# Two heads' score products on the two halves of the array's rows, operands split once for both heads

## The chip, the cores and the metric

One core of one Trainium2 chip runs the whole program. The metric is device microseconds of one execution. Five engines take part: TensorE (PE; its weight loads are shown as PEld), VectorE (DVE), ScalarE (ACT), GpSimd (POOL) and SyncE (SP), which issues the DMAs.

## What is computed

Three transformer-like layers over 512 tokens of width 1024, in float32. Two "hybrid" layers and one "second" layer:

```python
def hybrid_layer(x, ...):                      # twice
    u = rms_norm(x, g) @ w_in
    aq, ak, av, cu, rq, rk, rv, rg = split(u)
    y_att  = chunk_attention(aq, ak, av, rel_bias)   # 6 heads of 64
    y_conv = conv_module(cu, ...)                    # 31 taps over 256 channels
    y_ret  = retention(rq, rk, rv, rg)               # 6 heads of 64
    x = x + rms_norm(concat(y_att, y_conv, y_ret) @ w_out)
    return x + rms_norm(square(relu(rms_norm(x) @ w_up)) @ w_down)

def second_block(x, ...):                      # once
    q, k, v, u, gates = split(rmsnorm(x) @ w_in)
    o = diff_attention(q, k, v, lam)                 # 8 heads, two score maps of 64 each
    s = s5_layer(u, ...)                             # a state space model
    h = x + (g_attn * (o @ w_attn_proj) + g_ssm * (s @ w_ssm_proj)) @ w_out
    return h + (silu(gate) * val of causal_dwconv(rmsnorm(h) @ w_up)) @ w_down
```

A score map is the product of a head's queries and keys, a contraction over 64 features. There are 12 attention heads, 12 retention heads and 8 differential heads with two maps each: 40 maps, or 20 pairs.

## The kernel before

**Precision.** TensorE multiplies in its faster float32r format. To keep float32 accuracy, each operand is split into a high part, rounded to float32r by ScalarE (or VectorE), and a low part, the rest, made by VectorE (or GpSimd). A product over 128 features is three matmuls: high by high, high by low, low by high.

**Scores before.** A score map contracts over 64 features only, half of the array's 128 rows. `stack` (line 1060) puts a head's high parts in one half of the rows and its low parts in the other; `dup` (line 1076) writes the other operand's high parts into both halves of one tile and its low parts into both halves of another. Two matmuls over 128 rows then give all four products of a map. For a pair of heads `stack` makes two tiles (two ScalarE and two VectorE instructions on 64 partitions) and `dup` four tiles (four and four).

**Tiles of scores.** `att_head` (line 1167) handles one head: for each of four blocks of 128 queries, one PSUM tile with 256, 256, 384 and 512 columns, evicted by a VectorE instruction that adds the bias and takes the maximum; then exponentials, normalisation, transposes (`p_trans`), and the product with V (`pv_pair`). Two heads of a pair are separate tasks, the second put 1709 ns later (`ATTV`). `diff_head` (line 1790) does the same for the two maps of a head in one task. `ret_pair` (line 1279) does the two heads of a retention pair one after the other: for each, three PSUM tiles that hold 512, 384 and twice 256 columns.

**Order of the work.** The program is recorded first (`Trace`), each instruction with a due time, and a planner (`order`, line 443) then lays it out by simulated time. `cost` (line 682) gives it the duration of each instruction. Due times run back through the dependencies: an instruction is due before each user of its result, by that user's cost and 100 ns. Each engine takes the ready instruction that is due first. The main stream of projections has the due times of TensorE's own progress `T`. Scores, transposes and the like are side tasks (`Side`), created at the current `T`, and a `yield n` moves the due times of what follows by n. All side tasks share four PSUM tiles (`pss`, line 833), the main stream has four others. `room` (line 609) keeps enough of them for what stands earlier in the program. The planner's order is then fixed: each engine issues in that order and waits on semaphores. The matmuls of side tasks and of the main stream so share one queue on TensorE.

All instructions are issued through one line (642), so that the profile's groups are told apart by tile names: `stk`, `khi` and `klo` are the stacked and duplicated operands, `row` the scores, `pthi` and `ptlo` the split transposed probabilities, `whi` and `wlo` weights of the main stream, `ps` a PSUM tile, `cm` the identity of a transpose, `ucm` and `gt` operands of the state space model, which is computed with plain float32 matmuls over 64 rows.

Of the kernel before, what the change touches and what calls it, by code (L numbers as in the profile page):

```python
# [10 lines left out]
F32 = mybir.dt.float32  # L11
# [6 lines left out]
P = 128  # L18
S = 512
# [205 lines left out]
class View:  # L225
    """A view of a tile that is traced before the tile is placed."""
# [103 lines left out]
class DramView(View):  # L330
    """A view of a tile in DRAM: taken as a whole."""
# [20 lines left out]
class Pool:  # L352
    """Equal slots, which the order of instructions deals out to tiles. Each is a pool of one buffer."""
# [46 lines left out]
class Trace:  # L400
    """Records instructions with the time by which each is wanted, orders them, and issues them."""
# [280 lines left out]
def cost(eng, method, kw_, op):  # L682
# [6 lines left out]
    if eng == "tensor":  # L689
# [119 lines left out]
class Builder:  # L809
# [132 lines left out]
    # ---------------------------------------------------------------- norms  # L942
# [116 lines left out]
    # ---------------------------------------------------------------- attention helpers  # L1059
    def stack(self, ps, scale=None):  # L1060
        nc = self.nc
        out = []
        for e in range(2):
            t = self.s2(F32R, "stk")
            a, b = (slice(0, 64), slice(64, 128)) if e == 0 else (slice(64, 128), slice(0, 64))
            if scale is None:
                nc.scalar.copy(t[a, :], ps[a, :])
                nc.vector.tensor_tensor(t[b, :], ps[a, :], t[a, :].bitcast(F32), op=ALU.subtract)
            else:
                nc.scalar.activation(t[a, :], ps[a, :], AF.Copy, scale=scale)  # L1070
                nc.vector.scalar_tensor_tensor(t[b, :], ps[a, :], scale, t[a, :].bitcast(F32),
                                               op0=ALU.mult, op1=ALU.subtract)
            out.append(t)
        return out

    def dup(self, ps):
        nc = self.nc
        hs, ls = [], []
        for e in range(2):
            a = slice(64 * e, 64 * e + 64)  # L1080
            hi, lo = self.s2(F32R, "khi"), self.s2(F32R, "klo")
            for b in (a, slice(64 - 64 * e, 128 - 64 * e)):
                nc.scalar.copy(hi[b, :], ps[a, :])
            for b in (slice(0, 64), slice(64, 128)):
                nc.vector.tensor_tensor(lo[b, :], ps[a, :], hi[a, :].bitcast(F32), op=ALU.subtract)
            hs.append(hi)
            ls.append(lo)
        return hs, ls
# [12 lines left out]
    def v_pack(self, src):  # L1101
        """V of six heads, each as 64 columns of high parts and 64 of low parts."""
# [11 lines left out]
    def pv_pair(self, h, pts, V, y):  # L1114
        """One head's output, from the products with the high and the low parts of V below each other."""
# [24 lines left out]
    def p_split(self, parts):  # L1140
        """High and low parts by blocks of keys: 512, 384 and twice 256 columns, the last with a block of zeros."""
        out = []
        for src, off in parts:
            n = src.shape[1]
            hi, lo = self.s2(F32R, "pthi"), self.s2(F32R, "ptlo")
            if off:
                for z in (hi, lo):
                    self.nc.gpsimd.memset(z[:, :off].bitcast(F32), 0.0)
            self.split(src, hi[:, off:off + n], lo[:, off:off + n])
            out.append((hi, lo))  # L1150
        last = out.pop()
        return out + [tuple(z[:, 256:512] for z in last), tuple(z[:, 0:256] for z in last)]

    def p_trans(self, rows):
        nc = self.nc
        parts = []
        for kts, off in (((0,), 0), ((1,), 0), ((3, 2), P)):
# [6 lines left out]
            parts.append((ps[:, :n], off))  # L1164
        return self.p_split(parts)

    def att_head(self, l, h, q, khi, klo, toe, V, dst):
        nc = self.nc
        p, e = h // 2, h % 2
        st = self.st()  # L1170
        rows = self.rows(self.s2(name="row")[:, :256])
        for qt in range(NT):
            n = P * (qt + 1)
            N = max(n, 256)
            ps = self.ps()
            nc.tensor.matmul(ps[:, :N], q[:, qt * P:(qt + 1) * P], khi[:, :N], start=True, stop=False)
            nc.tensor.matmul(ps[:, :N], q[:, qt * P:(qt + 1) * P], klo[:, :N], start=False, stop=True)
            nc.vector.tensor_tensor_reduce(out=rows[qt][:, :n], in0=ps[:, :n], in1=toe[:, S - n:S], scale=1.0, scalar=-3e38,
                                           op0=ALU.add, op1=ALU.max, accum_out=st[:, qt:qt + 1])
        nc.vector.tensor_scalar(st[:, 4:8], st[:, 0:4], -1.0, None, op0=ALU.mult)  # L1180
        for qt in range(NT):
            n = P * (qt + 1)
            nc.scalar.activation(rows[qt][:, :n], rows[qt][:, :n], AF.Exp, bias=st[:, 4 + qt:5 + qt],
                                 accum_out=st[:, 8 + qt:9 + qt])
        yield 50
        nc.vector.reciprocal(st[:, 12:16], st[:, 8:12])
        for qt in range(NT):
            n = P * (qt + 1)
            nc.vector.tensor_scalar(rows[qt][:, :n], rows[qt][:, :n], st[:, 12 + qt:13 + qt], None, op0=ALU.mult)
        yield 50  # L1190
        pts = self.p_trans(rows)
        yield 50
        y, hi, lo = dst
        self.pv_pair(h, pts, V, y)
        self.mixc[p] = self.mixc.get(p, 0) + 1
        if self.mixc[p] == 2:
            self.split(y, hi, lo)
            self.mix[p] = hi, lo

    # ---------------------------------------------------------------- conv module  # L1200
# [48 lines left out]
    # ---------------------------------------------------------------- retention  # L1249
# [29 lines left out]
    def ret_pair(self, p, q, k):  # L1279
# [7 lines left out]
        ks = self.stack(pss[0])  # L1287
        qh, ql = self.dup(pss[1])
        yield 50
        y = self.s2(name="ry")  # L1290
        for e in range(2):
            h = 2 * p + e
            parts = []
            for kts in ((0,), (1,), (3, 2)):
                ps = self.ps()
                n = 0
                for kt in kts:
                    q0 = 256 if kt == 3 else P * kt
                    o = ps[:, n:n + S - q0]
# [780 lines left out]
```

## Time and profile before

| | |
|---|---|
| median of 3 executions | 2181.93 us (2181.4 to 2184.87) |
| profiled execution, first to last instruction | 2185.0 us |
| TensorE matmuls busy | 2065.8 us, 95% of the span |
| VectorE, ScalarE, GpSimd busy | 64%, 42%, 34% |
| mean granted TensorE clock | 0.983 of full speed |
| score matmuls (`khi,stk` and `klo,stk`) | 320 |

The profiled execution's own time is its span; no time around it is recorded. A matmul's shown duration is longer than its place in the queue, because matmuls overlap: where TensorE is saturated, the distance from one start to the next is the price. Retention and attention of the first hybrid layer lie between about 113 and 300 us, those of the second between 740 and 960 us, differential attention between 1430 and 1700 us.

### The profile page before, as it was taken

What the parts mean: (1) busy time and instruction counts of PE and PEld (TensorE: products, weight loads), DVE (VectorE), ACT (ScalarE), POOL (GpSimd) and SP (SyncE); (2) the same over time, 40 slices, a digit from 0 to 9 for tenths busy, and PEclk for the clock granted to TensorE, in tenths of its full rate; (3) what the DMA queues carried; (4) which work ended last, traced back from release to release, by engine and by line L of the source; (5) the groups of instructions that cost most, each with busy time, mean ns of one, the idle gap of its engine ahead of it and who ended that gap; (6) DMA issues with size and microseconds to landing.
All of it is one profiled execution on the core that took longest, in us unless ns stands there. A gap on an engine that the chain in (4) does not pass through costs nothing. (4 is left out here: it accounts for less than half of the span.)

```text
span 2185.0 us, 27033 instructions
## 1 busy us (share of the span) xinstructions
PE 2065.8 (95%) x9964; PEld 1711.6 (78%) x9964; DVE 1395.2 (64%) x2131; ACT 928.5 (42%) x1521; POOL 745.5 (34%) x858
## 2 busy tenths in 40 slices
PE   7789989899999799989999998999999999999999
PEld 7777878778888777788888877677777788888887
DVE  6999596344457999573444464379888646655545
ACT  3267544232234267454222344456578324433332
POOL 3663357980004663210000115764643431000000
PEclk9999999999999999999999999999999999999999
DMA  5223233332333224133332346222224533333222
GB/s 176 80 78 123 87 116 109 128 127 87 97 114 97 87 68 135 49 107 97 96 97 77 115 133 201 79 80 68 92 82 135 169 96 97 97 96 97 87 87 77
DMA packets 85556, 225.16 MB, mean 103 GB/s; under 512 B 10416, under 2 KB 20400, under 8 KB 85424
## 3 DMA queue, kind: packets, MB, share of 16 engines
q1 hardware_dynamic: 85424, 223.43, 32.4%
q8 instruction: 79, 1.29, 0.3%
q14 instruction: 53, 0.43, 0.1%
HBM read 204.25 MB, written 19.14 MB: 102 GB/s over the span
## 5 line engine op out<-in xcount | busy, mean ns | idle before, releaser
L642 POOL TENSOR_TENSOR wlo<-wraw,whi 128x1024 fp32r<-128x1024 f32 (+1 forms) x156 | 374.5, 2408 | 1068.3 <-ACT whi L642 824.9
L642 ACT CAST whi<-wraw 128x1024 fp32r<-128x1024 f32 (+1 forms) x323 | 330.4, 1029 | 726.7 <-PE ps L642 592.1
L642 PE MATMUL ps<-hhi,whi 128*128 128x512 f32 (+1 forms) x1488 | 506.8, 370 | 7.3 <-DVE acc L642 3.1
L642 PE MATMUL ps<-hlo,whi 128*128 128x512 f32 (+1 forms) x1488 | 504.8, 370 | 5.6 <-DVE hlo L642 5.6
L642 PE MATMUL ps<-hhi,wlo 128*128 128x512 f32 (+1 forms) x1488 | 504.3, 369 | 0.3 <-DVE wlo L642 0.3
L642 PEld LDWEIGHTS ps<-hhi,whi 128*128 128x128 f32 x1488 | 272.4, 191 | 54.8 <-issue 4.0
L642 PEld LDWEIGHTS ps<-hlo,whi 128*128 128x128 f32 x1488 | 272.4, 191 | 53.5 <-DVE hlo L642 6.8
L642 PEld LDWEIGHTS ps<-hhi,wlo 128*128 128x128 f32 x1488 | 272.1, 191 | 48.2 <-DVE wlo L642 1.0
L642 DVE TENSOR_TENSOR wlo<-wraw,whi 128x1024 fp32r<-128x1024 f32 x178 | 223.4, 1257 | 114.8 <-ACT whi L642 114.5
L642 PE MATMUL ps<-whi,fhi 128*128 128x512 f32 x688 | 249.7, 392 | 6.1 <-DVE t L642 3.7
L642 PE MATMUL ps<-whi,flo 128*128 128x512 f32 x688 | 249.5, 391 | 0.0
L642 PE MATMUL ps<-wlo,fhi 128*128 128x512 f32 x688 | 249.5, 391 | 0.0
L642 PE MATMUL ps<-wlo,hhi 128*128 128x384 f32 (+1 forms) x448 | 162.7, 380 | 18.3 <-POOL wlo L642 18.1
L642 DVE TENSOR_TENSOR acc<-ps,acc 128x512 f32<-128x512 f32 x112 | 76.5, 687 | 154.7 <-PE ps L642 154.7
L642 PE MATMUL ps<-whi,hhi 128*128 128x384 f32 (+1 forms) x448 | 161.7, 383 | 14.2 <-DVE rotb L642 12.7
L642 PE MATMUL ps<-whi,hlo 128*128 128x384 f32 (+1 forms) x448 | 158.8, 377 | 0.0
L642 PEld LDWEIGHTS ps<-whi,fhi 128*128 128x128 f32 x688 | 129.6, 189 | 34.7 <-DVE t L642 4.2
L642 PEld LDWEIGHTS ps<-wlo,fhi 128*128 128x128 f32 x688 | 129.6, 189 | 27.8
L642 PEld LDWEIGHTS ps<-whi,flo 128*128 128x128 f32 x688 | 129.5, 188 | 27.8
L642 DVE SCALAR_TENSOR_TENSOR cacc<-cy,pv,cacc 128x509 f32<-128x509 f32 (+26 forms) x120 | 125.3, 1088 | 0.6
L642 POOL TENSOR_TENSOR st<-st,mhalf 128x1 f32<-128x1 f32 (+1 forms) x56 | 54.9, 981 | 194.4 <-DVE st L642 190.8
L642 PEld LDWEIGHTS ps<-wlo,hhi 128*128 128x128 f32 x448 | 86.9, 195 | 30.6 <-POOL wlo L642 21.6
(250 smaller groups left out, 3167.8 us busy)
## 6 DMA issues: line engine op xcount, KB each, us to landing
wraw<-in_wst SPq DMA_DIRECT2D x302, 512.0 KB, 3.5
wraw<-in_wst SPq DMA_DIRECT2D x32, 384.0 KB, 3.1
gain<-in_gains SPq DMA_DIRECT2D x20, 256.0 KB, 4.2
X<-in_x SPq DMA_DIRECT2D x16, 256.0 KB, 6.1
xd<-X SPq DMA_DIRECT2D x16, 256.0 KB, 2.0
X<-xd SPq DMA_DIRECT2D x16, 256.0 KB, 4.9
gated<-t SPq DMA_DIRECT2D x16, 256.0 KB, 2.4
gate<-gated SPq DMA_DIRECT2D x16, 256.0 KB, 3.7
```

The source lines that it names most:

```text
L642: getattr(getattr(self.nc, e), m)(*[r(x) for x in op.args], **{k: r(v) for k, v in op.kw.items()})
```

## The change

The score operands of a pair are split as they stand, head 0 on partitions 0 to 63 and head 1 on 64 to 127, by one ScalarE and one VectorE instruction over 128 partitions for each operand (`two`). `pair_mm` issues the three products (high by high, high by low, low by high) of both heads, alternating between the heads; each matmul contracts over 64 rows, one head's on the upper and the other's on the lower half of the array. Low by low is dropped. Attention becomes one task for a pair (`att_pair`): scores of both heads, then exponentials of both, then normalisation, transposes and V product of one head after the other. Retention computes and splits the scores of both heads first. The planner takes 25 ns for a matmul on rows 64 to 127. Comments and blank lines are changed too, with no effect on the program.

```diff
@@ cost
         if method == "transpose":
             return 109.0
+        if lhs.p == (64, 128):
+            return 25.0
@@ instead of stack and dup
+    def two(self, ps, name, scale=None):
+        nc = self.nc
+        hi, lo = self.s2(F32R, name + "hi"), self.s2(F32R, name + "lo")
+        if scale is None:
+            nc.scalar.copy(hi, ps)
+            nc.vector.tensor_tensor(lo, ps, hi.bitcast(F32), op=ALU.subtract)
+        else:
+            nc.scalar.activation(hi, ps, AF.Copy, scale=scale)
+            nc.vector.scalar_tensor_tensor(lo, ps, scale, hi.bitcast(F32), op0=ALU.mult, op1=ALU.subtract)
+        return hi, lo
+
+    def pair_mm(self, outs, w, wc, x, xc):
+        for i, (a, b) in enumerate(((0, 0), (0, 1), (1, 0))):
+            for e in range(2):
+                r = slice(64 * e, 64 * e + 64)
+                self.nc.tensor.matmul(outs[e], w[a][r, wc], x[b][r, xc], start=i == 0, stop=i == 2)
@@ att_head becomes att_pair
+        rows = [self.rows(third[:, 256 * e:256 * (e + 1)]) for e in range(2)]
         for qt in range(NT):
             n = P * (qt + 1)
             N = max(n, 256)
-            ps = self.ps()
-            nc.tensor.matmul(ps[:, :N], q[:, qt * P:(qt + 1) * P], khi[:, :N], start=True, stop=False)
-            nc.tensor.matmul(ps[:, :N], q[:, qt * P:(qt + 1) * P], klo[:, :N], start=False, stop=True)
...
+            pss = [self.ps() for _ in range(2)]
+            self.pair_mm([ps[:, :N] for ps in pss], q, slice(qt * P, (qt + 1) * P), k, slice(0, N))
+            for e in range(2):
+                nc.vector.tensor_tensor_reduce(out=rows[e][qt][:, :n], in0=pss[e][:, :n], in1=toe[e][:, S - n:S], scale=1.0,
...
+        for e in range(2):
+            o = 16 * e
+            nc.vector.tensor_scalar(st[:, o + 4:o + 8], st[:, o:o + 4], -1.0, None, op0=ALU.mult)
+            for qt in range(NT):
+                r = rows[e][qt][:, :P * (qt + 1)]
+                nc.scalar.activation(r, r, AF.Exp, bias=st[:, o + 4 + qt:o + 5 + qt], accum_out=st[:, o + 8 + qt:o + 9 + qt])
+            yield 50
...
+        for e in range(2):
...
+            yield 50
+            pts = self.p_trans(rows[e])
+            yield 50
+            self.pv_pair(2 * p + e, pts, V, y)
+            yield self.ATTV
+        self.split(y, hi, lo)
+        self.mix[p] = hi, lo
@@ ret_pair
-        ks = self.stack(pss[0])
-        qh, ql = self.dup(pss[1])
+        k, q = self.two(pss[0], "k"), self.two(pss[1], "q")
...
+        for kts in ((0,), (1,), (3, 2)):
+            pss = [self.ps() for _ in range(2)]
+            n = 0
+            for kt in kts:
+                q0 = 256 if kt == 3 else P * kt
+                self.pair_mm([ps[:, n:n + S - q0] for ps in pss], k, slice(kt * P, (kt + 1) * P), q, slice(q0, S))
+                n += S - q0
+            for e in range(2):
+                parts[e].append(self.p_part(pss[e][:, :n], 0))
+            yield 50
@@ diff_head
-        q = self.stack(pss[0])
-        khi, klo = self.dup(pss[1])
+        q, k = self.two(pss[0], "q"), self.two(pss[1], "k")
...
+        for qt in range(NT):
+            n = P * (qt + 1)
+            N = max(n, 256)
+            pss = [self.ps() for _ in range(2)]
+            self.pair_mm([ps[:, :N] for ps in pss], q, slice(qt * P, (qt + 1) * P), k, slice(0, N))
```

## Rows read from the trace of the kernel before

**Rows 1.** The page's first part: busy us, share of the span, instructions.

```profile
PE 2065.8 (95%) x9964; PEld 1711.6 (78%) x9964; DVE 1395.2 (64%) x2131; ACT 928.5 (42%) x1521; POOL 745.5 (34%) x858
```

**Rows 2.** The stages with heads, by windows: length, then each engine's busy time.

```profile
core 0: us, PE busy (x) PEld busy (x) DVE busy (x) ACT busy (x) POOL busy (x), PEclk, DMA share, GB/s
113.00:240.00 127.00, 117.90 (x597) 97.78 (x596) 119.33 (x215) 92.06 (x178) 56.48 (x87) 0.97 0.27 92
240.00:300.00 60.00, 53.33 (x254) 44.99 (x253) 35.08 (x80) 25.88 (x52) 28.85 (x20) 0.94 0.41 128
740.00:915.00 175.00, 157.14 (x777) 132.45 (x778) 153.31 (x245) 105.41 (x194) 83.46 (x103) 0.95 0.29 94
915.00:960.00 45.00, 39.39 (x217) 33.98 (x216) 26.40 (x40) 18.86 (x44) 15.33 (x12) 0.96 0.28 94
1430.00:1700.00 270.00, 254.34 (x1222) 203.68 (x1221) 227.00 (x436) 180.69 (x335) 133.26 (x105) 1.00 0.31 96
```

**Rows 3.** TensorE's waits over the span: us in total, times, longest.

```profile
PE ps L642 <- DVE t L642: 20.5, 14, 3.7
PE ps L642 <- DVE rotb L642: 12.7, 6, 3.7
PE ps L642 <- DVE row L642: 11.7, 12, 2.1
PE ps L642 <- DVE klo L642: 6.2, 6, 1.5
```

**Rows 4.** Instructions that read or write the stacked and duplicated operands, duration min/median/max.

```profile
L642 PE MATMUL ps<-khi,stk x160: 276/336/796, 126.6 to 1662.1; 128*128 128x256 f32 x80, 128*128 128x512 f32 x40, 128*128 128x384 f32 x40
L642 ACT CAST stk<-ps x28: 566/580/583, 124.3 to 1645.7; 64x512 fp32r<-64x512 f32 x28
L642 DVE TENSOR_TENSOR stk<-ps,stk x28: 683/689/694, 125.9 to 1647.3; 64x512 fp32r<-64x512 f32 x28
...
L642 ACT CAST khi<-ps x80: 565/581/587, 113.1 to 1650.5; 64x512 fp32r<-64x512 f32 x80
L642 DVE TENSOR_TENSOR klo<-ps,khi x80: 671/688/696, 121.5 to 1657.8; 64x512 fp32r<-64x512 f32 x80
```

**Rows 5.** A split over 128 partitions, from the instructions around `yatt`.

```profile
L642 ACT CAST mixhi<-yatt x6: 612/620/622, 205.5 to 907.3; 128x512 fp32r<-128x512 f32 x6
L642 DVE TENSOR_TENSOR mixlo<-yatt,mixhi x6: 682/692/2312, 206.3 to 908.0; 128x512 fp32r<-128x512 f32 x6
```

**Rows 6.** TensorE in order of time, scores of a differential head among projections: start, us.

```profile
1456.88 0.33 PE L642 MATMUL ps<-klo,stk 128*128 128x384 f32 x1
1457.06 0.40 PE L642 MATMUL ps<-wlo,hhi 128*128 128x512 f32 x1
1457.29 0.40 PE L642 MATMUL ps<-whi,hhi 128*128 128x512 f32 x1
...
1458.21 0.28 PE L642 MATMUL ps<-khi,stk 128*128 128x256 f32 x1
1458.33 0.28 PE L642 MATMUL ps<-klo,stk 128*128 128x256 f32 x1
1458.45 0.40 PE L642 MATMUL ps<-whi,hlo 128*128 128x512 f32 x1
...
1459.38 0.60 PE L642 MATMUL ps<-cm,dqk 128*128 128x128 f32 x4
1459.74 0.48 PE L642 MATMUL ps<-whi,hlo 128*128 128x512 f32 x1
1460.06 0.39 PE L642 MATMUL ps<-wlo,hhi 128*128 128x512 f32 x1
```

**Rows 7.** The same view, where matmuls over 64 rows stand among projections.

```profile
1343.16 0.39 PE L642 MATMUL ps<-whi,hhi 128*128 128x512 f32 x1
1343.39 0.40 PE L642 MATMUL ps<-whi,hlo 128*128 128x512 f32 x1
1343.72 1.16 PE L642 MATMUL ps<-ucm,gt 64*128 64x128 f32 x8
1344.80 0.50 PE L642 MATMUL ps<-wlo,hhi 128*128 128x512 f32 x1
1345.14 0.39 PE L642 MATMUL ps<-whi,hhi 128*128 128x512 f32 x1
...
1384.94 0.40 PE L642 MATMUL ps<-wlo,hhi 128*128 128x512 f32 x1
1385.27 0.48 PE L642 MATMUL ps<-ucm,gt 64*128 64x128 f32 x2
1385.69 0.50 PE L642 MATMUL ps<-wlo,hhi 128*128 128x512 f32 x1
1386.03 0.40 PE L642 MATMUL ps<-whi,hlo 128*128 128x512 f32 x1
```

**Rows 8.** The same view, the last group of score matmuls.

```profile
1661.89 0.40 PE L642 MATMUL ps<-hhi,wlo 128*128 128x512 f32 x1
1662.12 0.28 PE L642 MATMUL ps<-khi,stk 128*128 128x256 f32 x1
1662.24 0.29 PE L642 MATMUL ps<-klo,stk 128*128 128x256 f32 x1
1662.37 0.39 PE L642 MATMUL ps<-hlo,whi 128*128 128x512 f32 x1
```

More of the change, by code (lines that the diff above doesn't have):

```diff
@@ L1138, in rows, with p_part, p_blocks @@
         return [a[:, 384:512], third, a[:, 0:384], b]
[L1140 to L1152, printed above, removed]
+    def p_part(self, src, off):
+        n = src.shape[1]
+        hi, lo = self.s2(F32R, "pthi"), self.s2(F32R, "ptlo")
+        if off:
+            for z in (hi, lo):
+                self.nc.gpsimd.memset(z[:, :off].bitcast(F32), 0.0)
+        self.split(src, hi[:, off:off + n], lo[:, off:off + n])
+        return hi, lo
+    def p_blocks(self, out):
+        last = out[-1]
+        return out[:-1] + [tuple(z[:, 256:512] for z in last), tuple(z[:, 0:256] for z in last)]
     def p_trans(self, rows):
@@ L1163, in p_trans, with att_pair @@
                     n += P
-            parts.append((ps[:, :n], off))
-        return self.p_split(parts)
-    def att_head(self, l, h, q, khi, klo, toe, V, dst):
+            parts.append(self.p_part(ps[:, :n], off))
+        return self.p_blocks(parts)
+    def att_pair(self, p, q, k, toe, V, dst):
         nc = self.nc
-        p, e = h // 2, h % 2
         st = self.st()
-        rows = self.rows(self.s2(name="row")[:, :256])
+        third = self.s2(name="row")
+        rows = [self.rows(third[:, 256 * e:256 * (e + 1)]) for e in range(2)]
         for qt in range(NT):
@@ L1181, in att_head @@
[L1181 to L1191, printed above, removed]
@@ L1340, in hybrid @@
         self.wbias = 2
-        self.mix, self.mixc, self.cacc, self.ry = {}, {}, {}, {}
+        self.mix, self.cacc, self.ry = {}, {}, {}
         def load_toe(p):
@@ L1395, in hybrid @@
             toe = load_toe(p)
-            self.f_unit(lambda ps: r.__setitem__("q", self.stack(ps, 0.125)))
-            self.f_unit(lambda ps: r.__setitem__("k", self.dup(ps)))
+            self.f_unit(lambda ps: r.__setitem__("q", self.two(ps, "q", 0.125)))
+            self.f_unit(lambda ps: r.__setitem__("k", self.two(ps, "k")))
             dst = (self.s2(name="yatt"), self.s2(F32R, "mixhi"), self.s2(F32R, "mixlo"))
-            for e in range(2):
-                self.side.add(self.att_head(l, 2 * p + e, r["q"][e], r["k"][0][e], r["k"][1][e], toe[e], V, dst), self.ATTV * e)
+            self.side.add(self.att_pair(p, r["q"], r["k"], toe, V, dst))
         for p in range(3):
@@ L1804, in diff_head @@
         rows = [self.rows(third[:, 256 * c:256 * (c + 1)]) for c in range(2)]
-        for c in range(2):
-            for qt in range(NT):
-                n = P * (qt + 1)
-                N = max(n, 256)
-                ps = self.ps()
-                lh = q[c][:, qt * P:(qt + 1) * P]
-                nc.tensor.matmul(ps[:, :N], lh, khi[c][:, :N], start=True, stop=False)
-                nc.tensor.matmul(ps[:, :N], lh, klo[c][:, :N], start=False, stop=True)
-                j = 4 * c + qt
-                nc.vector.tensor_tensor_reduce(out=rows[c][qt][:, :n], in0=ps[:, :n], in1=self.mask[:, S - n:S], scale=1.0,
-                                               scalar=-3e38, op0=ALU.add, op1=ALU.max, accum_out=st[:, j:j + 1])
+        for qt in range(NT):
+            n = P * (qt + 1)
+            N = max(n, 256)
+            pss = [self.ps() for _ in range(2)]
+            self.pair_mm([ps[:, :N] for ps in pss], q, slice(qt * P, (qt + 1) * P), k, slice(0, N))
+            for c in range(2):
+                j = 4 * c + qt
+                nc.vector.tensor_tensor_reduce(out=rows[c][qt][:, :n], in0=pss[c][:, :n], in1=self.mask[:, S - n:S], scale=1.0,
+                                               scalar=-3e38, op0=ALU.add, op1=ALU.max, accum_out=st[:, j:j + 1])
+        for c in range(2):
             sc = self.rq[:, p, 2 * hl + c, :]
```

59 lines of the change are left out of this document (8 added, 51 removed).

## Prediction

> **What bounds the kernel now.** I read the page's busy times first, then the windows of the stages that the change touches, TensorE's waits, the instructions on the operands that change, and last TensorE's queue instruction by instruction. TensorE is busy for 2065.8 of 2185.0 us [rows 1]; whatever lengthens its queue lengthens the kernel unless an idle stretch takes it up. In the stages with heads, five windows of 677 us, the reader is to subtract each PE column from its length: 9.1, 6.7, 17.9, 5.6 and 15.7 us, 55 us of idle TensorE in all [rows 2]. VectorE is busy for 561 us there: 94% of the first window (119 of 127 us), 88% of the window from 740 us and 84% of the one from 1430 us [rows 2]. The idle time is mostly TensorE waiting for VectorE results, of which only a part (`row`, `klo`) comes from heads; `t` and `rotb` are norms and rotations that the change leaves alone [rows 3].
>
> **The change part by part.**
>
> *Splits.* Before, the 20 pairs took 28 + 12 instructions for `stk` and 80 for `khi`/`klo` on each of the two engines (the 12 scaled ones are taken at the time of the 28) [rows 4]. ScalarE: 40 x 0.58 + 80 x 0.581 = 69.7 us; VectorE: 40 x 0.689 + 80 x 0.688 = 82.6 us. After, 40 instructions on each over 128 partitions, at 0.62 and 0.69 us [rows 5]: 24.8 and 27.7 us. ScalarE is relieved of 45 us, VectorE of 55 us, 10% of its 561 us in these stages. This is off TensorE's queue. It is worth at most the 55 us of idle time. I take half of that, 27.5 us: the waits for `row` and `klo` and the load on VectorE shrink, those for rotations and norms don't have to. Bounds: 0 and 45 us.
>
> *Streaming on TensorE.* In a full queue a matmul of 512 columns takes 0.23 us and one of 256 takes 0.12 (start to start), 384 takes 0.18 [rows 6]. A head's four tiles, 256, 256, 384 and 512 columns, cost 0.65 us per product over them; I call that a stream. Before, a pair takes two heads by two products, 4 streams or 2.6 us, over 20 pairs 52 us. After, there are 6 streams, each on half of the rows. If two matmuls on different halves run together and the two heads always alternate, that is 3 streams in time: 20 x 0.65 = 13 us less. If they run one after the other, it is 6: 26 us more. The trace has no two row halves in use at once, so both ends stand.
>
> Which it is hangs on the planner. The recorded order alternates, but the planner reorders by due time. Two things pull the heads apart. A second head's matmul is put at 25 ns, so the second of three products is due 125 ns before the third, while for the first head it is due by 0.2 to 0.3 us earlier; with all operands ready the order is first head, first head, second head, second head, first head, second head, in which two of the six overlap pairs and the sum is 4 streams. In `att_pair` the second head's softmax, transposes and V product are due 1809 ns later (50 + 50 + `ATTV` after the first's), and due times run back, so that its scores are due that much later than all of the first head's. And the four PSUM tiles of side tasks come free one by one, as VectorE evicts them. The reader sees the result in the trace of before: one tile's two matmuls, then a projection, then the next tile's [rows 6]. A tile alone has no partner. I take 5 streams: 20 x 0.65 = 13 us more. Bounds -13 and +26 us.
>
> *Going in and out of 64 rows.* The trace has matmuls over 64 rows, `ucm,gt`, in the queue of projections [rows 7]. Read it so: from the start of the projection ahead (1384.94) to the start of the second one behind (1386.03) there are 1.09 us. The two projections account for 0.46. A group of eight lasts 1.16 us, one of two 0.48, so that six more cost 0.68 us, 0.113 each, and the two here account for 0.23. 0.40 us is left. The group of eight gives 1.75 - 0.46 - 0.90 = 0.39 [rows 7]. It shows twice on each side: the first matmul behind a change starts 0.33 us instead of 0.23 after the last, and the next one again about 0.1 us late. It is not the number format: four float32 transposes over 128 rows among projections take 1459.38 to 1460.06, 0.68 us [rows 6], and 4 x 0.113 + 0.23 is 0.68. So a visit to 64 rows costs 0.40 us, however short. Before, scores are over 128 rows and cost no visit.
>
> How many visits: before, the 320 score matmuls stand in 136 groups with other matmuls between, the first at 126.6 us and the last at 1662.1 us [rows 4, 8], on 148 PSUM tiles (48 in attention, 64 differential, 36 retention by the code). The number of tiles and of PSUM slots stays, the evicting instructions too. A first burst into free slots can take several tiles in one visit, the rest follow as slots come free. I take 100 visits, 40 us. Bounds: 60 (three a pair: two fills of the slots and one disturbance), 24 us; 148 (each tile alone), 59 us.
>
> *Other parts.* Holding the scores of both heads takes more SBUF tiles at once; the pool has 55 and the price lies in waits, which I put at 0 (between -5 and +10 us: the relief of six operand tiles to four, against a stall a pair like the 1.5 us longest for `klo` [rows 3] in seven of the 20). DMAs, GpSimd's masks, exponentials and evictions are the same in number and size, and SyncE's queue is not passed by anything. In retention the first head's masks and V product now stand behind the second head's scores in the record, 0.65 us x 3 a pair; nothing but the pair's own result waits for them, and it is used only in the output projection, so nothing is put down.
>
> *Sum.* +13 + 40 - 27.5 = +25.5 us on the profiled execution, 2185.0 to 2210.5 us. Its span lies 3.1 us above the median of the three executions, so on that 2181.9 + 25.5 = 2207 us. What is late next is TensorE's own queue in the three stages with heads.
>
> **The rivals.**
>
> *Relief wins (faster).* Place: the 55 us of idle TensorE. The heads stay adjacent (3 streams, -13), the visits are 60 (+24) and half of the idle time goes (-27.5): -16.5 us, 2165 us. It decides from the point where visits and streams cost less than the idle time given back: at 4 streams and 27.5 us, below 69 visits. For it: VectorE's load in the first window, 119 of 127 us [rows 2], and a burst of three products a tile that lasts longer than two. Against: each eviction that the next tile waits for lets a projection in [rows 6]. If besides the price of a visit did not hold for float32r, it would be -13 - 27.5, 2141 us; nothing in the rows says so, and this far end is left out of the range. The Trainium skill, page "TensorE: Matmul & The Clock Gate", Part 3 (Measured speedup vs the span model), has matmuls in different row groups start about 4 ns apart and run together. That is this rival's 3 streams, if the heads are adjacent; no run here shows it yet, and without the visits it would be the -13 us above alone.
>
> *Nothing pairs (much slower).* Each tile is alone: 6 streams (+26), 148 visits (+59), 27.5 us given back: +57.5 us, 2239 us. For it: the slots freed one by one [rows 6]. Against: bursts when the operands become ready.
>
> *It cancels (same).* 4 streams and 69 visits, within 4 us of 2182. A crossing between the first two rather than a place of its own.
>
> **How the numbers follow.** Forecast, 2186 to 2226 us: 0.49. Relief wins: 0.27. Nothing pairs, above 2226 us: 0.15. It cancels: 0.09. A measurement of this kernel can tell about 0.2%, 4.4 us, from no change. Faster 0.27, same 0.09, slower 0.64. The range goes from 2160 (relief's 2165 and a little more idle time given back) to 2240 us (nothing pairs); since both signs have weight, the forecast's own range is 2186 to 2226.
>
> **What would show it.** Score matmuls appear 480 times with 64 rows. Right on the visits: a projection behind a score group starts about 0.1 us late and the one after it again. Right on the order: most groups hold matmuls of one head only, or pairs of the same head in a row. If two matmuls of different halves start a few ns apart, halves run together; if they start a full 0.12 or 0.23 us apart, they don't. Splits: 40 each on ScalarE and VectorE, busy 45 and 55 us lower. The five windows' idle TensorE time should fall from 55 to about 27 us. The prediction is wrong if there are fewer than 69 groups, if a visit costs much less than 0.4 us, or if the idle time falls by more than the visits cost.

## The result, and the profile after

The changed kernel takes 2242.4 us (median of 4 runs, 2238.6 to 2245.7) beside 2183.4 us of the kernel before (2181.4 to 2189.3): a ratio of 1.0267, 95% interval 1.0249 to 1.0286. It is 59 us slower. The forecast was 2207 us, +25.5: the sign was right, the size was not, and the time lies 2.4 us above the upper end of the range. The two profiled executions, from which all rows come, have spans 54.9 us apart (2239.9 and 2185.0).

First the page's busy times, as in [rows 1]: TensorE has 66.9 us more work, VectorE 38 and ScalarE 53 us less. TensorE's share stays at 95%.

```profile
PE 2132.7 (95%) x10124; PEld 1739.7 (78%) x10124; DVE 1356.9 (61%) x2047; ACT 875.8 (39%) x1438; POOL 746.9 (33%) x859
```

Then the stages with heads, as in [rows 2], but with the ends moved to where the same projections stand; the two hybrid layers have one window each.

```profile
core 0: us, PE busy (x) PEld busy (x) DVE busy (x) ACT busy (x) POOL busy (x), PEclk, DMA share, GB/s
113.00:320.70 207.70, 190.56 (x894) 150.25 (x893) 144.46 (x272) 100.51 (x204) 83.81 (x106) 0.94 0.28 93
760.70:997.60 236.90, 218.46 (x1041) 177.36 (x1042) 162.58 (x260) 104.68 (x209) 98.41 (x115) 0.93 0.27 87
1467.60:1754.80 287.20, 275.54 (x1281) 209.28 (x1281) 213.31 (x398) 163.69 (x305) 133.99 (x105) 0.98 0.29 91
```

Before, these stages were 187, 220 and 270 us long. They grow by 20.7, 16.9 and 17.2 us, 54.8 in all; between and behind them nothing moves. Subtract the PE column from the length: 17.1 + 18.4 + 11.7 = 47.2 us of idle TensorE, against 55 before. TensorE's busy time rises from 622.1 [rows 2] to 684.6 us. PEclk is to be read too: the mean granted clock is 0.94, 0.93 and 0.98, against 0.96, 0.95 and 1.00 over the same work.

TensorE's waits, as in [rows 3] (us in total, times, longest): `row` and `klo`, which come from heads, did not give the relief that I counted on (16.2 us, 17.9 before). The growth of `t` is none of the change: its 7.7 us are TensorE's first wait of the program, which before (8.0 us) was put down to the DMA of `cm`. In the three stages alone the waits for `t` are 5.3 us, and were 6.8.

```profile
PE ps L642 <- DVE t L642: 27.0, 15, 7.7
PE ps L642 <- DVE row L642: 12.2, 7, 2.9
PE ps L642 <- DVE rotb L642: 11.2, 5, 4.2
PE ps L642 <- DVE klo L642: 4.0, 2, 2.8
```

The instructions on the operands, as in [rows 4]: 20 splits of each kind over 128 partitions, at the prices of [rows 5], and score matmuls with 64 rows (two of the six groups are shown).

```profile
L642 PE MATMUL ps<-khi,qhi x112: 275/384/790, 179.8 to 1708.7; 64*128 64x256 f32 x56, 64*128 64x512 f32 x28, 64*128 64x384 f32 x28
L642 PE MATMUL ps<-qhi,khi x48: 275/382/497, 125.4 to 835.0; 64*128 64x256 f32 x24, 64*128 64x512 f32 x12, 64*128 64x384 f32 x12
L642 ACT CAST khi<-ps x20: 573/594/622, 124.4 to 1695.8; 128x512 fp32r<-128x512 f32 x20
L642 DVE TENSOR_TENSOR klo<-ps,khi x20: 629/680/693, 125.0 to 1696.5; 128x512 fp32r<-128x512 f32 x20
```

TensorE in order of time, where the two heads' operands had just become ready. The first two matmuls start 10 ns apart: they are on different halves and run together. The next two are 0.24 us apart.

```profile
126.44 0.50 PE L642 MATMUL ps<-qhi,khi 64*128 64x512 f32 x1
126.45 0.50 PE L642 MATMUL ps<-qhi,klo 64*128 64x512 f32 x1
126.78 0.39 PE L642 MATMUL ps<-qlo,khi 64*128 64x512 f32 x1
127.02 0.39 PE L642 MATMUL ps<-qhi,klo 64*128 64x512 f32 x1
```

And the usual picture, one head's three matmuls alone among projections, to be read as [rows 7]: from 131.95 to 133.22 there are 1.27 us, of which three score matmuls and two projections of 384 columns account for 5 x 0.174 = 0.87. The visit to 64 rows costs 0.40 us.

```profile
131.95 0.34 PE L642 MATMUL ps<-whi,hhi 128*128 128x384 f32 x1
132.22 0.44 PE L642 MATMUL ps<-qhi,khi 64*128 64x384 f32 x1
132.50 0.33 PE L642 MATMUL ps<-qlo,khi 64*128 64x384 f32 x1
132.68 0.33 PE L642 MATMUL ps<-qhi,klo 64*128 64x384 f32 x1
132.94 0.44 PE L642 MATMUL ps<-whi,hhi 128*128 128x384 f32 x1
133.22 0.34 PE L642 MATMUL ps<-wlo,hhi 128*128 128x384 f32 x1
```

Over the whole trace there are 109 such groups, 51 of them of exactly three matmuls and 21 of six. Of the 47 groups of three that can be read between projections the median is 0.406 us: 109 x 0.406 = 44.3 us. Of 371 starts inside groups 71 stand beside a partner on the other half and save 11.1 us (57 to 80 starts and 7 to 11 us, by how close two starts must be to count); the matmuls' own time is 76.1 us, before it was 50.7: 76.1 - 11.1 - 50.7 = +14.3 us.

What the prediction had not looked for is this (PEclk is the third number from the end; the first line is of the timeline, with the wait in brackets):

```profile
184.95 1.01 PE L642 MATMUL ps<-klo,qhi 64*128 64x512 f32 x2 [2.75 <-DVE klo L642]
180.00:185.00 5.00, 2.25 (x11) 1.40 (x11) 4.89 (x5) 1.37 (x2) 2.37 (x1) 1.00 0.17 64
185.00:190.00 5.00, 5.00 (x17) 3.50 (x17) 1.95 (x9) 0.00 (x0) 0.00 (x0) 0.51 0.11 44
190.00:195.00 5.00, 5.00 (x12) 3.05 (x12) 1.81 (x9) 2.29 (x8) 0.00 (x0) 0.50 0.00 0
195.00:200.00 5.00, 5.00 (x16) 3.90 (x15) 1.08 (x3) 2.67 (x9) 2.39 (x1) 0.63 0.01 2
...
864.30:874.60 10.30, 10.30 (x26) 7.00 (x27) 3.12 (x15) 4.33 (x9) 2.37 (x1) 0.50 0.01 2
```

TensorE waited 2.75 us for `klo`; behind that the clock stands at the lower of its two levels (1.2 instead of 2.4 GHz) for 13.7 us; short visits with projections between them fill the first 9, projections alone the rest. A projection of 512 columns then takes 0.43 us from start to start instead of 0.23. The second such stretch is the last line: 10.2 us, in a burst of score visits that began after a wait of 1.2 us for `klo`. These two are the only stretches at the lower level with score matmuls in them. Together they are 23.9 us, in which 12 us of work are lost; the other stretches at that level, some 88 us of the span, hold no scores.

### The profile page after: what moved, and what is told of

It is laid out like the page before. It is cut to its first block, busy times and chain, and to the rows that moved or that the text cites. A ratio compares the mean times of both kernels' runs of the same rounds, so it can differ in the third digit from the quotient of the medians.

```text
span 2239.9 us, 27115 instructions
## 1 busy us (share of the span) xinstructions
PE 2132.7 (95%) x10124; PEld 1739.7 (78%) x10124; DVE 1356.9 (61%) x2047; ACT 875.8 (39%) x1438; POOL 746.9 (33%) x859
## 5 line engine op out<-in xcount | busy, mean ns | idle before, releaser
L642 PE MATMUL ps<-hhi,whi 128*128 128x512 f32 (+1 forms) x1488 | 517.3, 375 | 6.3 <-DVE acc L642 3.1
L642 PE MATMUL ps<-hlo,whi 128*128 128x512 f32 (+1 forms) x1488 | 514.1, 373 | 5.3 <-DVE hlo L642 5.3
L642 PE MATMUL ps<-hhi,wlo 128*128 128x512 f32 (+1 forms) x1488 | 514.0, 373 | 0.2 <-DVE wlo L642 0.2
L642 PE MATMUL ps<-wlo,hhi 128*128 128x384 f32 (+1 forms) x448 | 161.0, 386 | 17.3 <-POOL wlo L642 17.2
L642 PEld LDWEIGHTS ps<-wlo,hhi 128*128 128x128 f32 x448 | 87.2, 197 | 31.4 <-POOL wlo L642 19.9
```

What stands on the lines that cost most here:

```text
L642: getattr(getattr(self.nc, e), m)(*[r(x) for x in op.args], **{k: r(v) for k, v in op.kw.items()})
```

## The experiments

Each time is compared with the kernel before on the same chip; the intervals are 95%.

### One part alone: only the relief, only the joint tasks

**relief.** The kernel before with its operands split once for both heads, two products over all 128 rows. The scores aren't the heads' own; the time is meant.

```diff
 def stack(self, ps, scale=None):
...
-            out.append(t)
-        return out
+    return self.two(ps, "q", scale)
 def dup(self, ps):
...
-        return hs, ls
+    hi, lo = self.two(ps, "k")
+    return [hi, hi], [lo, lo]
```

> The kernel before, in which only the splits change: each operand of a pair is split once over 128 partitions, and the two products of a head stay matmuls over 128 rows (4 streams, no visits to 64 rows). The rearrangement of the halves is left out, so the scores are not those of the heads. Measures by itself what 45 us less ScalarE and 55 us less VectorE work are worth. Theory A (the loss is in TensorE's queue: 109 visits at 0.41 us, two extra streams of which part overlaps, little idle time given back): 8 to 16 us faster than before, 2167 to 2175 us. My recorded term (half of the idle time comes back): 27 us faster, 2156 us. Theory B (the joint tasks for two heads delay the chains behind the scores): no statement here but the same 8 to 27 us.

Measured: 2161.0 beside 2185.7 us, ratio 0.9897 (0.988 to 0.9913): -24.7 us, against -27.5 in my sum and -8 to -16 in theory A. Its page:

```profile
PE 2052.9 (95%) x9964; PEld 1710.8 (79%) x9964; DVE 1334.5 (62%) x2044; ACT 881.6 (41%) x1444; POOL 747.9 (35%) x860
```

The span is 2159.0 us, so the idle time is 106.1 us against 119.2 before. That is half of the gain; the other 12.9 us are busy time of TensorE, with the same matmuls. The granted clock of the two profiled executions (0.985 against 0.983) would be some 5 us of it, but the other three executions of relief had 0.983 too and two of them took the same time. So where the 12.9 us lie stays open.

**struct128.** The changed kernel, with its tasks that hold both heads, but two products over 128 rows; the scores aren't the heads' own.

```diff
 def pair_mm(self, outs, w, wc, x, xc):
-    for i, (a, b) in enumerate(((0, 0), (0, 1), (1, 0))):
-        for e in range(2):
-            r = slice(64 * e, 64 * e + 64)
-            self.nc.tensor.matmul(outs[e], w[a][r, wc], x[b][r, xc], start=i == 0, stop=i == 2)
+    for e in range(2):
+        for b in range(2):
+            self.nc.tensor.matmul(outs[e], w[e][:, wc], x[b][:, xc], start=b == 0, stop=b == 1)
```

> The changed kernel with its joint tasks and single splits, but each head's scores as two products over 128 rows (4 streams, no visits); the scores are not those of the heads. Against the changed kernel it takes away visits, extra products and overlap at once, against the run with the splits alone it adds the joint tasks. Theory A: within 5 us of the run with the splits alone, 2165 to 2180 us. Theory B (joint tasks cost 20 us or more, through SBUF room and later first results): 2195 us or more.

Measured: 2172.8 beside 2185.7 us, ratio 0.9944 (0.9929 to 0.9959). It differs from relief by the joint tasks alone, and they cost 11.8 us, more than the 5 of theory A and less than the 20 of theory B. Its page:

```profile
PE 2062.4 (95%) x9964; PEld 1714.9 (79%) x9964; DVE 1342.2 (62%) x2044; ACT 876.3 (40%) x1440; POOL 746.1 (34%) x860
```

With a span of 2170.8 us the idle time is 108.4 us, 2.3 more than in relief. The rest is busy time of TensorE with the same number of matmuls, so no wait that the profile shows explains it.

**mix.** relief with the joint tasks in retention and differential attention, and attention's heads as separate tasks; against struct128 the edit is

```diff
-    self.side.add(self.att_pair(p, r["q"], r["k"], toe, V, dst))
+    for e in range(2):
+        self.side.add(self.att_head(l, 2 * p + e, ...), self.ATTV * e)
```

> As the run with the splits alone (2 products over 128 rows, scores not those of the heads), with the joint order of two heads taken over in retention and differential attention, while attention keeps two tasks. Tells where the 12 us lie that separate the joint tasks from the splits alone. If attention's joint task costs them: 2161 to 2166 us; if retention's and differential attention's joint order: 2170 to 2175 us; half each: 2167 us.

Measured: 2166.0 beside 2184.9 us, ratio 0.991 (0.9894 to 0.9927). Some 3 to 5 of the 11.8 us lie in the order of retention and differential attention and about 7 in attention's joint task; differences of so few us are near what the runs can tell.

### The third product, and the row halves

**six128.** The changed kernel, each of the three products over all 128 rows: 6 streams, no visits. The scores aren't the heads' own.

```diff
-            r = slice(64 * e, 64 * e + 64)
-            self.nc.tensor.matmul(outs[e], w[a][r, wc], x[b][r, xc], start=i == 0, stop=i == 2)
+            self.nc.tensor.matmul(outs[e], w[a][:, wc], x[b][:, xc], start=i == 0, stop=i == 2)
```

> The changed kernel with three products a head over 128 rows: the same 480 score matmuls in the same program, 6 streams, no 64 rows, no visits; the scores are not those of the heads. Theory A: 25 us slower than the run with two products over 128 rows (2 streams by 20 pairs), so 2190 to 2205 us, 37 to 52 us faster than the changed kernel: visits 44 us and clock 8 us gone, overlap of 11 us lost. Theory B: 2215 us or more. Theory C (the lower granted clock, not the visits, makes the loss): the time at half clock falls from 113 us back to 70 to 80 us and the gain over the changed kernel is about half of that, 20 us: 2220 us.

Measured: 2195.7 beside 2185.7 us, ratio 1.0056 (1.0038 to 1.0074). Two more streams than struct128 cost 22.9 us (20 x 2 x 0.65 = 26 by the prediction's price). The changed kernel is 46.7 us slower than this one, though it streams less: that is what going over to halves costs, the planner's 25 ns included.

**halves.** A program of its own: dense float32r matmuls, and among them matmuls over 64 rows in several orders.

```
low      60 x [half 0]                      512 columns
alt      60 x [half 0, half 1]              512 columns
quarter  60 x [half 0, half 1]              256 columns
lone     20 x [3 x half 0 (256), 1 dense]
six      16 x [3 x (half 0, half 1), 1 dense]
order    16 x [half 0, 0, 1, 1, 0, 1]      512 columns
```

> A program of its own, not the computation: one float32r matmul repeated, in stretches with a tile name each, with stretches of 128 rows by 512 columns (dense) between them. Expected by theory A, start to start at full clock: dense 0.23 us; low (60 over the lower 64 rows, 512 columns) 0.23 each; alt (60 pairs, one on each half, 512 columns) 0.23 a pair; quarter (60 pairs of 256 columns) 0.12 a pair if the weight loads of the halves overlap too, 0.21 if they take turns; lone (20 times three of 256 columns on one half, then one dense) 0.23 + 3 x 0.12 + 0.41 = 0.99 us a time; six (16 times six alternating of 512 columns, then one dense) 0.23 + 3 x 0.23 + 0.41 = 1.33 us a time; order (16 times the order lower, lower, upper, upper, lower, upper) 4 x 0.23 = 0.92 a time. Rival: the halves take turns, alt 0.46 a pair. On the clock: theory C says it falls in the low or the lone stretch and stays at full in alt and six; if it stays at full speed everywhere, matmuls over 64 rows alone don't lower it.

The windows of the six stretches in this order:

```profile
29.80:43.60 13.80, 13.80 (x61) 10.97 (x60) 0.00 (x0) 0.00 (x0) 0.00 (x0) 1.00 0.00 0
57.50:71.30 13.80, 13.80 (x121) 11.14 (x120) 0.00 (x0) 0.00 (x0) 0.00 (x0) 1.00 0.01 1
85.20:92.50 7.30, 7.30 (x121) 7.21 (x120) 0.00 (x0) 0.00 (x0) 0.00 (x0) 1.00 0.01 2
106.30:125.40 19.10, 19.10 (x80) 11.81 (x79) 0.00 (x0) 0.00 (x0) 0.00 (x0) 1.00 0.00 1
139.40:160.30 20.90, 20.90 (x112) 10.55 (x111) 0.00 (x0) 0.00 (x0) 0.00 (x0) 1.00 0.00 0
174.40:185.50 11.10, 11.10 (x97) 9.44 (x96) 0.10 (x1) 0.00 (x0) 0.00 (x0) 1.00 0.01 1
```

60 matmuls on one half take 13.8 us, and 120 that alternate take the same: a pair costs 0.229 us, as one. A period of lone lasts 0.975 us; less 0.229 and 3 x 0.116 this leaves 0.40 us a visit. Six matmuls in alternation cost 0.41 us a visit. So price and overlap are as the prediction had them, and the clock stays at 1.00 here, visits included (clockgap shows that this is not always so). One expectation failed: order takes 0.69 us a time and not 0.92, since in the repeated stretch the last matmul of one group starts beside the first of the next. What a single group in this order costs, 4 streams by my reckoning, no run shows. The Trainium skill, page "TensorEngine Tiling (Array Packing)", Key Properties, says that changing the tiling mode drains TensorE and gives no price. The 0.40 us a visit here agree with that; no row shows the drain itself.

### The order of the planner

**costfix.** The changed kernel without the lines that put a matmul over 64 rows at 25 ns.

```diff
-        if lhs.p == (64, 128):
-            return 25.0
```

> The changed kernel without its 25 ns for matmuls on the upper rows: the planner gives them the price of any matmul, so that in retention and differential attention the products of both heads are due at the same times and alternate. Theory A: more pairs overlap (some 20 us saved in place of 11), the number of visits stays at 100 to 115: 5 to 12 us faster than the changed kernel, 2230 to 2238 us. Rival: the planned price is the cause that the heads stand apart, and with it right they alternate nearly everywhere, overlap saves 38 us: 2215 us.

Measured: 2211.0 beside 2184.9 us, ratio 1.0114 (1.0099 to 1.0129), 31.4 us faster than the changed kernel. I had expected 5 to 12. The rival's 2215 us were near, but not its reason: the overlap did not rise to 38 us. Spans and clocks of the changed kernel and of this one:

```profile
core 0: 2239.9 us, clock 0.975
```

```profile
core 0: 2207.2 us, clock 0.982
```

There are 86 visits instead of 109 (23 x 0.406 = 9.3 us) and 16.4 us of overlap instead of 11.1 (5.3 us). No stretch at the lower clock holds score matmuls any more. The time at the lower clock is 2 x (1 - clock) x span: 112 us against 79 (the kernel before: 74). At that level half of the work is lost, so the difference is worth up to 16.5 us by the two profiled executions and 12 by the mean clocks of four (0.981 against 0.976); the three make 27 to 31. The score matmuls stand in 86 groups in six128 too, of the same sizes, so that the 15.3 us from there to here are the halves alone: 86 x 0.406 = 34.9 for visits, less 16.4 of overlap, is 18.5.

**group1.** The changed kernel with the six matmuls of a pair of tiles as one unit of the planner, so that they stay adjacent and alternate.

```diff
 def pair_mm(self, outs, w, wc, x, xc):
-    for i, (a, b) in enumerate(((0, 0), (0, 1), (1, 0))):
...
+    self.group([(outs, w, wc, x, xc)])
...
 def cost(op):
+    if op.plan:
+        return 400.0 + 3 * sum(max(0.4222 * p[0].n, 107.0) + 2.5 for p in op.plan[::6])
```

> The changed kernel, all of it computed, but the six matmuls of a pair of score tiles are one unit for the planner, which it puts down alternating between the heads and without anything between (80 units, with the two of a last retention part apart 86 at most), at a planned cost of three streams and 400 ns. Theory A: all pairs overlap (3 streams, 38 us in all against 65) and at most 86 visits (35 us against 44): 25 to 40 us faster than the changed kernel, 2203 to 2217 us. Theory B: no more than 10 us faster, since the joint tasks stay. Theory C: the half-clock time decides; if it stays at 113 us the gain is that of the streams alone, 27 us or less.

Measured: 2195.7 beside 2185.7 us, ratio 1.0052 (1.0037 to 1.0067): 46.7 us faster than the changed kernel, more than I expected, and as fast as six128. There are 69 visits (28.0 us), 237 of 411 starts inside groups have a partner, and 37.6 us of streaming are saved; the clock is 0.981. The unit also replaces the 25 ns by a price of its own, so what keeping the six together gives by itself is rather the distance to costfix, 15.3 us.

**group2.** As group1, with two pairs of tiles to a unit: 12 matmuls and four PSUM tiles.

```diff
-            self.pair_mm([ps[:, :N] for ps in pss], q, slice(qt * P, (qt + 1) * P), k, slice(0, N))
+                for t in (qt, qt + 1):
...
+                    jobs.append(([ps[:, :N] for ps in tiles[t]], q, slice(t * P, (t + 1) * P), k, slice(0, N)))
+                self.group(jobs)
```

> All of the computation. As the run with units of one pair of score tiles, but a unit holds two pairs (four PSUM tiles, twelve matmuls alternating between the heads), two units a pair of heads, 40 visits at most. Theory A (a visit costs 0.41 us whatever is in it, adjacent halves overlap): against the run with units of one pair, 34 visits or so fewer, 14 us faster: 2178 to 2184 us, that is 2 to 8 us faster than before. Theory B (the PSUM tiles of the side tasks are the limit; a unit that needs all four at once waits and holds other side tasks up): no gain over the units of one pair or a loss, 2195 us or more.

Measured: 2222.0 beside 2184.9 us, ratio 1.0169 (1.0153 to 1.0184). Theory B had this. There are only 40 visits, and the streams overlap as in group1, but waits grow (us in total, times, longest; in group1 `row` is 13.9 us and `xlo` 4.3):

```profile
PE ps L648 <- DVE row L648: 17.7, 8, 5.3
PE ps L648 <- DVE xlo L648: 8.8, 7, 2.4
```

TensorE's idle time is 21 us more than in group1 (2224.5 - 2090.6 = 133.9 against 2193.0 - 2080.0 = 113.0). The clock is 0.970, the lowest of all, which is 133 us at the lower level against 83 there, 25 us of work. Both together exceed the 12 us of the 29 visits saved. That it is the four free PSUM tiles at once for which a unit waits is my reading; no row shows it.

### The clock

**clockgap.** A program of its own, with 45 dense matmuls of 512 columns ("wide") four times, and four times 12 visits of three matmuls with a projection between ("visit"), each behind work of VectorE that TensorE was to wait for (`gap`).

```
for n in range(4):
    gap();  45 x dense;  60 x dense
    gap();  12 x [3 x half 0 (256), 1 dense];  60 x dense
```

> A program of its own on the granted clock: four times a wait of about 4 us of TensorE for VectorE and then 45 matmuls over 128 rows by 512 columns (wide), and four times the same wait and then 12 times three matmuls of 64 rows by 256 columns and one over 128 rows by 512 (visit), each followed by 60 dense ones. If a wait puts the clock to half and matmuls over 128 rows bring it back at once while visits hold it down, as the changed kernel's stretch from 185 to 199 us suggests, the half-clock time is 3 to 7 us in each wide stretch and 10 us or more in each visit stretch. Rival: visits don't matter, only the wait does: the same 3 to 7 us in both.

The waits were not the same. Each wide stretch stands behind 3.9 us of idle TensorE. No visit stretch does: VectorE was done (118.27 us for the second) before the dense matmuls ahead were, and TensorE went on from them without a pause.

```profile
117.84 0.43 DVE L52 CAST mvisitb<-slow 128x512 fp32r<-128x512 f32 x1
111.75 6.73 PE L40 MATMUL ps<-mdense,wt 128*128 128x512 f32 x29
118.42 0.61 PE L46 MATMUL ps<-mvisitb,wt 64*128 64x256 f32 x3
```

So the run can't compare visits with dense matmuls behind a wait. It shows something else. Windows of two wide stretches, then of the first three visit stretches, then the second of these in two parts:

```profile
32.60:45.90 13.30, 13.26 (x46) 10.71 (x47) 0.00 (x0) 0.00 (x0) 0.00 (x0) 0.78 0.00 0
88.70:100.80 12.10, 12.09 (x46) 9.84 (x47) 0.00 (x0) 0.00 (x0) 0.00 (x0) 0.86 0.01 1
...
63.50:75.20 11.70, 11.70 (x50) 7.41 (x50) 0.00 (x0) 0.00 (x0) 0.00 (x0) 1.00 0.00 0
118.40:134.60 16.20, 16.20 (x50) 10.10 (x50) 0.00 (x0) 0.00 (x0) 0.00 (x0) 0.67 0.00 1
179.90:196.20 16.30, 16.30 (x50) 10.11 (x50) 0.00 (x0) 0.00 (x0) 0.00 (x0) 0.66 0.00 0
...
118.40:123.80 5.40, 5.40 (x24) 3.41 (x23) 0.00 (x0) 0.00 (x0) 0.00 (x0) 1.00 0.00 0
123.80:134.60 10.80, 10.80 (x27) 6.69 (x27) 0.00 (x0) 0.00 (x0) 0.00 (x0) 0.50 0.01 2
```

At the full clock the 46 dense matmuls of a wide window would take 46 x 0.229 = 10.5 us, so the wait costs them 1.6 to 2.8 us more than its own length. The visits take 11.7 us at the full clock, which they had once, and 16.2 or 16.3 us three times: 4.5 us more. In these three the clock was full for the first five or six visits and then fell to the lower level, with no wait before and TensorE busy throughout. So visits by themselves can bring the clock down; they did in three stretches of four here, and not in the 20 visits of halves. Why the first stretch here and that one stayed at the full clock is open.

### Versions that could beat both

**dma_all.** Everything is computed: the kernel before, each head a task of its own, with two products over 128 rows; operands split once, then stacked and duplicated by 12 DMAs a pair on SyncE's queue.

```diff
 def dup(self, ps):
+    for z, name in zip(self.two(ps, "n"), ("khi", "klo")):
+        for e in range(2):
+            t = self.s2(F32R, name)
+            for h in range(2):
+                self.move(t[64 * h:64 * h + 64, :], z[64 * e:64 * e + 64, :])
```

(and the stacked operand in the same way)

> All of the computation, without 64 rows: the kernel before with its two products over 128 rows, each operand split once over 128 partitions, and the stacked and duplicated tiles put together from it by 12 DMAs a pair of 64 partitions by 512 columns (128 KB each, 31 MB over the kernel, 14% more than before). ScalarE and VectorE keep the full relief of 45 and 55 us. Theory A (the relief was worth 25 us, and what lies behind the splits can wait): 8 to 22 us faster than before, 2163 to 2177 us; the DMAs' 2 to 4 us of latency before the scores cost the difference to the 25. Rival: the DMAs hold up the weight loads in SyncE's queue, and scores come late: no gain or slower.

Measured: 2194.4 beside 2184.9 us, ratio 1.0043 (1.0031 to 1.0056). The rival was right in that the scores come late: TensorE waits for the copies, which land 2.2 to 7.9 us after their issue. That they hold up weight loads does not show (TensorE's waits for `wlo` are 17.1 us, before 18.1).

```profile
PE ps L642 <- DMA klo<-nlo: 11.1, 13, 2.1
PE ps L642 <- DMA khi<-nhi: 9.7, 8, 1.9
```

**dma_k.** The same, heads as separate tasks, with the stacked operand written by ScalarE and VectorE as in the kernel before; only the duplicated one goes by DMA, eight a pair.

> The same with the duplicated operand alone put together by DMAs (8 a pair), the stacked one as before: half of the relief (27 us ScalarE, 28 us VectorE: 3 instructions a pair in place of 6 on each). Theory A: half the gain, 4 to 12 us faster than before, 2173 to 2181 us. Rival (latency and queueing of the DMAs decide): as much or more than the other run.

Measured: 2172.7 beside 2184.9 us, ratio 0.9946 (0.9933 to 0.996). It beats both kernels and computes everything. The waits for copies are down to this:

```profile
PE ps L642 <- DMA klo<-nlo: 5.9, 11, 1.0
```

**dma_sep.** The kernel before with only `dup` replaced by that of dma_k. It was meant as dma_k without the joint tasks, but dma_k has none: the two are the same program, with TensorE's 9964 matmuls in the same order.

> The kernel before with one edit: the duplicated operand of a pair is split once over 128 partitions and its four copies are written by eight DMAs on SyncE's queue; the stacked operand, the order of the two heads and two products over 128 rows stay as before. Everything is computed. Theory A (the relief of ScalarE and VectorE and the joint tasks are separate terms: what the joint tasks cost, 5 to 12 us by mix and struct128 against relief, comes back when the heads are left as separate tasks): 2161 to 2168 us, ratio 0.989 to 0.993. Rival (in dma_k the DMAs' latency of 2 to 8 us already sets the end, and the order of the heads only moves which wait it is): 2171 to 2175 us, ratio 0.994 to 0.996.

Measured: 2171.4 beside 2185.2 us, ratio 0.9944 (0.993 to 0.9957). So this is dma_k once more, 1.3 us apart. It decides between neither theory, and joint tasks with operands put together by DMA were not run.

## Why the prediction was right in sign and wrong in size

*By the runs.* Each step is the difference of two medians: relief -24.7, joint tasks +11.8, two more streams +22.9, halves instead of whole rows +46.7. The sum, 56.7 us, is the distance of the changed kernel from the 2185.7 us of the kernel before in that call. costfix cuts the last step in two: +15.3 with the planner's usual price, and +31.4 for the 25 ns. My sum had -27.5, 0 and +53 (40 + 13) where the runs have -24.7, +11.8 and +69.6: the tasks and the halves, third product included, are where it failed.

*By the trace.* In the stages with heads TensorE's idle time falls by 7.7 us and its busy time rises by 62.5. Visits (44.3) and streams (14.3) are 58.6 of that. The clock of the three windows means 70 us at the lower level against 37 before, so some 16 us of work more, 12 of them in the two stretches with score visits. All three are 12 us too much, about the busy time that relief lost as well; I take it for the same, without proof.

*Visits: right.* 100 of 0.40 us, 40 us, were predicted; 109 of 0.406, 44.3 us, were found, and the same price in halves. *Streams: right.* 5 in time, +13, were predicted; +14.3 were found. Matmuls on different halves do run together (3 to 4 ns apart in alt of halves), and the heads were mostly pulled apart, as I said.

*Splits and idle time: right alone, not in the whole.* The relief by itself is worth 24.7 us (27.5 predicted). In the changed kernel the idle time of the stages fell to 47.2 us and not to 27: the waits for `row` and `klo` stayed (16.2 of 17.9 us). [rows 3] covers the whole span, and I read it for the stages: only 6.8 of its 20.5 us for `t` lie there.

*The step that failed first: "which I put at 0".* The tasks that hold both heads cost 11.8 us, above the +10 that I had allowed them. Mix puts some 3 to 5 us of it in retention and differential attention and about 7 in attention. By struct128 it is for the most part not idle time, where I had looked for it, but busy time of TensorE; what lengthens that is not settled.

*The step that was missing: the clock.* The sum had no term for it. The kernel before spent 74 us at the lower clock, the changed one 112; (112 - 74) / 2 = 19 us over the whole span, 16 in the stages. 12 of these are the two stretches with score visits; costfix has no such stretch. With them the step from whole rows to halves adds up: 44.3 for visits, 12 for the clock, less 11.1 of overlap, is 45 us of the 46.7 measured. clockgap shows visits bring the clock down without a wait, though not each time; in the changed kernel both stretches also stood behind a wait for `klo`, so how much is the wait's there is not shown.

*The 25 ns.* I read them as what pulls the heads apart and priced that in streams alone (5 instead of 3). By costfix they decide on 31.4 us, of which the overlap is only 5; more visits and a longer time at the lower clock make up most of the rest. "Relief wins" described the halves as they could be, but group1, with the pairs adjacent and 69 visits, still does not beat the kernel before: my break-even of 69 visits left out the joint tasks and the clock. "Nothing pairs" gave 2239 us, next to the measured time, for a wrong reason: 71 starts had partners, and there were 109 visits, not 148.

## What to carry to other kernels

A matmul over half of the rows costs its visit first (0.40 us here, more than one 512-column matmul): halves pay where they alternate in long runs, and not three matmuls at a time among work over 128 rows. A price given to a planner sets an order, so an order's visits belong in the sum, and so does what visits can do to the clock; when a relief and a new cost come in one change, price the relief alone, and look for a way to have it without the cost, as the eight DMAs a pair did here.

## What the runs showed of the hardware

- Alternating halves also overlap at 256 columns: 120 matmuls in 7.3 us, 0.12 us a pair, with a weight load for each (7.21 us of loads in that window).
- A visit costs 0.40 us for three matmuls of one half and 0.41 for six in alternation, for float32r in a program of its own; in this kernel the median of 47 visits of three is 0.406.
- Visits can lower the clock by themselves: with no wait before, 12 visits took 16.2 us three times, at the lower level from the sixth or seventh on, and 11.7 once; 20 visits in halves stayed at 1.00. Dense matmuls lost 1.6 to 2.8 us behind a wait of 3.9 us (clockgap).
- Copies from SBUF to SBUF landed 2.2 us after their issue at best and 2.3 in the median; the latest took 7.9 us with 12 a pair (dma_all) and 4.6 with eight (dma_sep).
